# A decoder layer on one core: prompt scores in plain fp32, and four smaller edits on TensorE's way

## The chip, the cores and the metric

The kernel runs on one core of a Trainium2 chip. The metric is the device time of one execution in microseconds (us). A core has the engines TensorE (PE; its weight loads are listed as PEld), VectorE (DVE), ScalarE (ACT), GpSimd (POOL) and SyncE (SP); the last two here mostly issue DMAs. PSUM is the memory that PE writes to, SBUF the one that it reads from.

## What is computed

One layer of a hybrid decoder over 256 prompt rows and 8 x 8 sample rows (T = 320 rows in all), D = 2048, in fp32:

```python
xn = rms_norm(x, g_mix)
z = xn @ w_in                      # B, C, h, q, k, v, gate_conv, gate_attn
u = C * h;  y_A = (B * conv3(u)) @ w_conv_out
s = (q . k) * HEAD_DIM**-0.5 + rel_bias[t5_bucket(dist)]    # 16 heads, 4 key heads, window 128
p = softmax(s with a sink per head);  y_B = (p . v) @ w_attn_out
h = x + (sigmoid(gate_conv) * y_A + sigmoid(gate_attn) * y_B) @ w_o
h = h + (silu(hn @ w_gate) * (hn @ w_up)) @ w_down          # hn = rms_norm(h, g_ffn), D_FF = 5632
y = rms_norm(h, g_final)
```

It also returns the last keys and values and the state of the convolution.

## The kernel before, in words

Activations lie with features on the partitions and the 320 rows along the free axis. Each weight arrives by SP in blocks of 512 KB (`wraw`), ACT rounds it to fp32r (`whi`), and DVE takes the difference (`wlo`; `split_to`, L127 to L130). A product is then three fp32r matmuls: high by high, high by low, low by high (`product`, L176). The moving rows are read in a turned order, four at a time (`turns`, L101); the order in which the three kinds follow each other is set by `passes`.

Work beside the products comes from a generator, `side_work`, which takes one step after each weight block (`tick`), and from a list, `pending`, whose entries are put behind a block's split and matmuls.

The places that the change touches, in the order of the program:

- *The norms' sums.* `two_rows` splits a row of sums of squares into two fp32r parts and `over_partitions` (L197 to L199) adds them over the partitions with two matmuls, both with the weights `ones_r` and both in the turned order: into `prb` for the first norm, into `pss` for the second. A `nudge` (L193 to L195) is a matmul whose result nobody uses; it reads its rows in one piece. One follows the second norm's sum by way of `pending`, two stand in the sample attention, one in the first product.
- *Prompt scores.* `keys_twice` (L773) writes high and low parts of each key head to both halves of the partitions (`k2`), and `q_out` (L793) writes for each query chunk two tiles, with the high part on one half and the low part on the other (`q2`, in `at_t`). `prompt_scores` (L537) then makes, for a key head and two query heads (one of 8 `units`), six fp32r matmuls of 256 columns over all 128 partitions (L548 and L551) into `ps1` and `ps0`, and DVE adds the bias. `prompt_weights` (L627) runs the units two ticks apart.
- *First 128 rows of the output.* In the second half of the last product, `down` (L1023) makes three columns of 512 features: per weight set (two chunks of 128) eight matmuls of 512 columns `dn` with `whi`, two rows `dl` for the low part of the first 128 activations, and eight matmuls of 320 columns with `wlo`. Afterwards `rows_of` (L1120) turns the first 128 rows of a column by four PE transposes (`fa`, L1124), adds the low part `ylow`, sums squares and multiplies by `gfb`; `rest_of` takes the other 192 rows. Both are put in `pending` behind each column.
- *Last column.* Its weights are held. L1178 to L1200 make the products of the other rows, 384 columns with `whi` (L1191) and 320 with `wlo` (L1196), and every second set takes an entry of `pending`. DVE then adds the results (L1212, L1213, L1219, L1224) and sums squares into `yacc` (L1217, L1220). The first 128 rows are made with rows as weights, into `rowacc` (L1231); between them stand `pn` (L1235), which sums `yacc` over the partitions, and four transposes of `hT` (L1238). From `pn` ACT and DVE make the factor and seven products (L1248) for the output of the other rows, and from `rowacc` those of the first.

Of the kernel before, what the change touches and what calls it, by code (L numbers as in the profile page):

```python
# [21 lines left out]
WIN = 128  # L22
# [30 lines left out]
def hybrid_layer(ctx: ExitStack, tc: tile.TileContext, a: dict, o: list):  # L53
# [133 lines left out]
    def two_rows(src, hi, lo):  # L187

        nc.scalar.activation(hi, fives(src), AF.Copy)
        nc.vector.tensor_sub(lo, fives(src), hi.bitcast(F32))  # L190
        return hi, lo
# [240 lines left out]
    def first_norm():  # L432
# [5 lines left out]
        parts = two_rows(xacc, at_h(7), at_l(7))  # L438
# [37 lines left out]
    k2 = pr.tile([P, NKV, 2, TP], F32R, name="k2")  # L476
    k2h, k2l = k2[:, :, 0], k2[:, :, 1]

    def q2(ch, par):
        o = LEAD_A + ch * at_row + par * TP  # L480
        return at_t[:, o:o + TP]

# [54 lines left out]
    def prompt_scores(kv, gp, bias):  # L537

        j, par = kv // 2, kv % 2
# [15 lines left out]
        p0 = ps0.rearrange("p (g two k) -> p g two k", g=2, two=2)  # L558
        nc.vector.tensor_add(s[:, 0:2], p0[:, :, 0], flip(bias[:, :, 0:WIN]))
        nc.vector.tensor_add(s[:, 0:2], p0[:, :, 1], s[:, 0:2])  # L560
# [66 lines left out]
    def prompt_weights(scrs):  # L627
        bias, sc, sm = {}, {}, {}
        bias[0] = bias_load(*units[0])
        for i in range(len(units) + 1):  # L630
            if i < len(units):
                if i + 1 < len(units):
                    bias[i + 1] = bias_load(*units[i + 1])
                sc[i] = prompt_scores(*units[i], bias.pop(i))
                yield
                sm[i] = prompt_softmax(*units[i], sc[i])
# [136 lines left out]
    def keys_twice():  # L773
        for kv in range(NKV):
# [563 lines left out]
```

## Time and profile before

| | us |
|---|---|
| median of 3 runs | 1594.37 (1593.99 to 1594.84) |
| the profiled execution | 1594.48 |
| its span, first to last instruction | 1592.8 |
| PE busy | 1584.2 (99%), 11296 matmuls, granted clock 0.998 |
| DVE, ACT, POOL busy | 882.6 (55%), 650.2 (41%), 125.3 (8%) |
| DMA | 166 GB/s in the mean |

Busy time of PE is counted from modelled ends of pipelined matmuls, so that neighbours overlap; the time from one start to the next is the price of a matmul in a row. A plain fp32 matmul leaves two records in the trace, an fp32r one leaves one.

### The profile page before, as it was taken

The page shows a single profiled execution, that of the slowest core. Times are in us where ns is not written, and L with a number is a line of the kernel's source. Part 1 is how long each engine was busy: PE and PEld are TensorE (multiplying, and loading weights), DVE is VectorE, ACT ScalarE, POOL GpSimd, SP SyncE. Part 2 cuts the span into 40 slices and gives each one's busy share as a digit, 9 for nine tenths or more (in the row PEclk, how much of TensorE's full clock was granted, in tenths as well). Part 3 has the DMA queues.
Part 4 walks back from the last instruction along what each step waited for, and adds up shares of the span by engine and source line. Part 5 has one row for each costly group of instructions (what it writes and reads, how often), then busy time and mean ns, then how long its engine had stood idle before and what let it go on. Part 6 is the DMA issues. An engine that isn't in the chain of part 4 may idle for free.

```text
span 1592.8 us, 27120 instructions
## 1 busy us (share of the span) xinstructions
PE 1584.2 (99%) x11296; PEld 1569.0 (99%) x11296; DVE 882.6 (55%) x1258; ACT 650.2 (41%) x901; POOL 125.3 (8%) x214
## 2 busy tenths in 40 slices
PE   9999999999999999999999999999999999999998
PEld 9999999999999999999999999999999999999887
DVE  7889765455444455565555555553444455555556
ACT  7555344333333333444333333333333343344443
POOL 2223342000000003320000000000000000000000
PEclk9999999999999999999999999999999999999999
DMA  8666666444444444444444444455555544445652
GB/s 274 205 188 194 214 188 217 156 156 158 159 159 154 157 157 156 159 159 156 156 155 157 159 159 159 155 153 158 158 159 159 159 155 156 155 158 159 185 173 93
DMA packets 77090, 264.51 MB, mean 166 GB/s; under 512 B 9576, under 2 KB 13000, under 8 KB 76840
## 3 DMA queue, kind: packets, MB, share of 16 engines
q1 hardware_dynamic: 71880, 249.86, 49.3%
q0 software_dynamic: 4656, 12.25, 2.5%
q8 instruction: 88, 1.44, 0.4%
q10 hardware_dynamic: 432, 0.69, 0.1%
q14 instruction: 34, 0.28, 0.1%
HBM read 256.46 MB, written 8.26 MB: 166 GB/s over the span
## 4 chain that ended last, share of the span: by engine, by line
PE 99%; ACT 0%; DVE 0%; DVEq 0%; issue 0%
PE fu L176 19%; PE fg L176 19%; PE dn L1015 12%; PE wo L176 7%; PE ga L176 7%; PE gc L176 7%; PE q L176 3%; PE B L176 3%; PE H L176 3%; PE C L176 3%; PE ya L176 3%; PE yc L176 3%; PE dn L1040 3%; PE dn L1048 2%; PE kv L371 2%; PE dl L1044 1%
## 5 line engine op out<-in xcount | busy, mean ns | idle before, releaser
L130 DVE TENSOR_TENSOR wlo<-wraw,whi 128x1024 fp32r<-128x1024 f32 (+1 forms) x460 | 562.4, 1223 | 580.1 <-ACT whi L129 569.4
L129 ACT ACTIVATE whi<-wraw 128x1024 fp32r<-128x1024 f32 (+1 forms) x460 | 485.1, 1056 | 713.0 <-PE fu L176 131.9
L176 PE MATMUL fu<-hh_t,whi 128*128 128x320 f32 x704 | 205.1, 301 | 0.0
L176 PE MATMUL fu<-hl_t,whi 128*128 128x320 f32 x704 | 205.0, 301 | 0.0
L176 PE MATMUL fg<-hh_t,whi 128*128 128x320 f32 x704 | 205.0, 301 | 0.0
L176 PE MATMUL fg<-hl_t,whi 128*128 128x320 f32 x704 | 205.0, 301 | 0.0
L1015 PE MATMUL dn<-a_t,whi 128*128 128x320 f32 x896 | 162.6, 301 | 0.0
L176 PE MATMUL fu<-hh_t,wlo 128*128 128x320 f32 x704 | 158.8, 301 | 0.0
L176 PE MATMUL fg<-hh_t,wlo 128*128 128x320 f32 x704 | 158.8, 301 | 0.0
L1015 PEld LDWEIGHTS dn<-a_t,whi 128*128 128x128 f32 x896 | 137.5, 187 | 0.0
L176 PEld LDWEIGHTS fu<-hl_t,whi 128*128 128x128 f32 x704 | 131.7, 187 | 0.0
L176 PEld LDWEIGHTS fu<-hh_t,whi 128*128 128x128 f32 x704 | 131.6, 187 | 0.0
L176 PEld LDWEIGHTS fg<-hh_t,whi 128*128 128x128 f32 x704 | 131.6, 187 | 0.0
L176 PEld LDWEIGHTS fg<-hl_t,whi 128*128 128x128 f32 x704 | 131.6, 187 | 0.0
L176 PEld LDWEIGHTS fu<-hh_t,wlo 128*128 128x128 f32 x704 | 116.1, 187 | 0.0
L176 PEld LDWEIGHTS fg<-hh_t,wlo 128*128 128x128 f32 x704 | 116.1, 187 | 0.0
L1015 PE MATMUL dn<-a_t,wlo 128*128 128x320 f32 x448 | 103.9, 301 | 0.0
L1015 PEld LDWEIGHTS dn<-a_t,wlo 128*128 128x128 f32 x448 | 74.8, 187 | 0.0
L176 PE MATMUL gc<-xh_t,whi 128*128 128x320 f32 x256 | 74.5, 301 | 0.0
L176 PE MATMUL gc<-xl_t,whi 128*128 128x320 f32 x256 | 74.5, 301 | 0.0
L176 PE MATMUL ga<-xh_t,whi 128*128 128x320 f32 x256 | 74.5, 301 | 0.0
L176 PE MATMUL ga<-xl_t,whi 128*128 128x320 f32 x256 | 74.5, 301 | 0.0
(319 smaller groups left out, 2811.0 us busy)
## 6 DMA issues: line engine op xcount, KB each, us to landing
wraw<-in_w_in_dram SPq DMA_DIRECT2D x128, 512.0 KB, 3.7
wraw<-in_w_gate_dram SPq DMA_DIRECT2D x88, 512.0 KB, 3.6
wraw<-in_w_up_dram SPq DMA_DIRECT2D x88, 512.0 KB, 3.6
wraw<-in_w_down_dram SPq DMA_DIRECT2D x88, 512.0 KB, 3.6
wraw<-in_w_o_dram SPq DMA_DIRECT2D x32, 512.0 KB, 3.6
wraw<-in_w_conv_out_dram SPq DMA_DIRECT2D x16, 512.0 KB, 3.7
wraw<-in_w_attn_out_dram SPq DMA_DIRECT2D x16, 512.0 KB, 3.7
wraw<-in_w_kv_dram SPq DMA_DIRECT2D x6, 512.0 KB, 7.7
```

What stands on the lines that cost most here:

```text
L129: last["hi"] = nc.scalar.activation(hi, src, AF.Copy)
L130: last["lo"] = nc.vector.tensor_sub(lo, src, hi.bitcast(F32))
L176: last["mm"] = nc.tensor.matmul(turns(fives(ps[c][:, :T])), w[:, k, c * P:(c + 1) * P], turns(x(kc)), start=(kc == 0 and i == 0), stop=(kc ...
L371: last["mm"] = nc.tensor.matmul(turns(fives(ps[c][:, :T])), w[:, k, c * P:(c + 1) * P], turns(x(kc)), start=(kc == 0 and m == 0), stop=(kc ...
L1015: last["mm"] = nc.tensor.matmul(turns(fives(ps[c][:, :T])), parts[k][w][:, c * P:(c + 1) * P], turns(x(k)), start=k == 0 and m == 0, stop= ...
L1040: nc.tensor.matmul(turns(placed(ps[c])), parts[k][0][:, cs], turns(a_move(k)), start=k == 0, stop=False)
L1044: nc.tensor.matmul(low, a_low(k), parts[k][0], start=k == 0, stop=k == nf - 1)
L1048: last["mm"] = nc.tensor.matmul(turns(placed(ps[c])[:, :, 0:JT]), parts[k][1][:, cs], turns(a_move(k)[:, :, 0:JT]), start=False, stop=k == ...
```

## The change

- `over_partitions` reads the low part in one piece, from a plain stretch of 320 columns that is lent by `at_t` or `a_t` (`a_fives` returns it as a third value). The `nudge` behind the second norm goes.
- The prompt scores become plain fp32. `q_out` writes the scaled query once (`qf`), `keys_twice` goes (four empty steps keep the others in place), and `prompt_scores` makes two key heads at once: the heads lie on partitions 0 to 63 and 64 to 127 of `kT` and `qf`, their matmuls alternate and go to separate PSUM tiles. Four groups of eight matmuls take the place of eight groups of six. `prompt_biased` adds the bias, and a `nudge` follows the last group one tick later.
- `rows_turn` turns the first 128 rows of a column on DVE in blocks of 32 and takes them through DRAM by five POOL DMAs (four writes of 64 KB, one read of 256 KB) straight to `y0`; `rows_of` only adds `ylow`. The columns of `ylow`, `g_final` and the output are permuted to match, the last two on the host. `pending` gets three entries a column, and the last column takes one at every even set.
- In the last column all sets but the final one run all matmuls with `whi` first and then those with `wlo`.

```diff
     def two_rows(src, hi, lo):
...
-        nc.vector.tensor_sub(lo, fives(src), hi.bitcast(F32))
+        nc.vector.tensor_sub(fives(lo), fives(src), hi.bitcast(F32))
...
     def over_partitions(out, parts):
-        for i, x in enumerate(parts):
-            nc.tensor.matmul(turns(fives(out)), ones_r, turns(x), start=i == 0, stop=i == 1)
+        hi, lo = parts
+        nc.tensor.matmul(turns(fives(out)), ones_r, turns(hi), start=True, stop=False)
+        nc.tensor.matmul(out, ones_r, lo, start=False, stop=True)
...
-        parts = two_rows(xacc, at_h(7), at_l(7))
+        parts = two_rows(xacc, at_h(7), at_t[:, LEAD_A + 6 * at_row:LEAD_A + 6 * at_row + T])
...
-    def prompt_scores(kv, gp, bias):
...
-        ps1, ps0 = ps_aux(u("ps1")), ps_aux(u("ps0"))
-        for gi in range(2):
-            q = q2(j * 4 + gp * 2 + gi, par)
-            for i in range(2):
-                nc.tensor.matmul(
-                    ps1[:, gi * 256:(gi + 1) * 256], q[:, WIN:2 * WIN], k2[:, kv, i], start=i == 0, stop=i == 1
-                )
-            nc.tensor.matmul(
-                ps0[:, gi * 256:(gi + 1) * 256].rearrange("p (two k) -> p two k", two=2), q[:, 0:WIN],
-                k2[:, kv, :, 0:WIN], start=True, stop=True,
-            )
+    def prompt_scores(j, gp):
+
+        both = [(ps_aux(u("ps1")), ps_aux(u("ps0"))) for _ in range(2)]
+        for gi in range(2):
+            q = qf[:, j * 4 + gp * 2 + gi]
+            for b, n in ((0, WIN), (1, 2 * WIN)):
+                for par, (ps1, ps0) in enumerate(both):
+                    rows = slice(par * 64, par * 64 + 64)
+                    nc.tensor.matmul(
+                        (ps1 if b else ps0)[:, gi * n:(gi + 1) * n], q[rows, b * WIN:(b + 1) * WIN],
+                        kT[rows, j, 0:n], start=True, stop=True,
+                    )
+        return both
...
         for i in range(len(units) + 1):
             if i < len(units):
...
+                if i % 2 == 0:
+                    both[i], both[i + 1] = prompt_scores(units[i][0] // 2, units[i][1])
+                sc[i] = prompt_biased(*both.pop(i), bias.pop(i))
+                if i + 2 < len(units):
+                    bias[i + 2] = bias_load(*units[i + 2])
                 yield
+                if i == len(units) - 2:
+                    nudge(xh, xl, T)
                 sm[i] = prompt_softmax(*units[i], sc[i])
...
-        yield from keys_twice()
+        for _ in range(4):
+            yield
...
-            t = tmp("ta", "qt")[:, :TP]
-            nc.vector.tensor_mul(t, ps[c][:, :TP], rbq[:, :TP])
-            for par in range(2):
-                r0, o0 = par * 64, 64 - par * 64
-                q = q2(j * 4 + g, par)
-                nc.scalar.activation(q[r0:r0 + 64], t[r0:r0 + 64], AF.Copy)
-                nc.vector.tensor_sub(q[o0:o0 + 64], t[r0:r0 + 64], q[r0:r0 + 64].bitcast(F32))
+            nc.vector.tensor_mul(qf[:, j * 4 + g], ps[c][:, :TP], rbq[:, :TP])
...
-        nc.scalar.activation(ylow[:, c0:c0 + 512], low, AF.Copy)
+        nc.scalar.activation(
+            ylow[:, c0:c0 + 512].rearrange("p (a k j) -> p k a j", a=4, k=4),
+            low.rearrange("p (k a j) -> p k a j", k=4, a=4), AF.Copy,
+        )
...
-                over_partitions(pss[:, :T], two_rows(hacc, a_hi(FH[0] - 1), a_lo(FH[0] - 1)))
+                over_partitions(pss[:, :T], two_rows(hacc, a_hi(FH[0] - 1), a_spare))
                 rstd_of(pss[:, :T], [P, T], "r2", hp, out=rb2)
-                pending.append(lambda: nudge(hh, hl, P))
...
+            def rows_turn(c0):
+
+                flipped = op.tile([P, 512], F32, tag="jk", name=u("yT")).rearrange("p (b k j) -> p b k j", b=4, k=4)
+                nc.vector.transpose(
+                    flipped.rearrange("p b k j -> p k b j"),
+                    hT[:, c0 // P:c0 // P + 4, 0:P].rearrange("p k (b i) -> p k b i", i=B),
+                )
+                rows = turned_rows(f"y_scr{c0}", flipped.rearrange("p b k j -> p (b k j)"), 4, 4 * B)
+                nc.gpsimd.dma_start(y0[:, c0:c0 + 512], rows)
+
             def rows_of(c0):
 
-                pt = ps_aux(u("fa"))
-                for c in range(4):
-                    nc.tensor.transpose(pt[:, c * P:(c + 1) * P], hT[:, c0 // P + c, 0:P], ident)
                 y = y0[:, c0:c0 + 512]
-                nc.vector.tensor_add(y, pt, ylow[:, c0:c0 + 512])
+                nc.vector.tensor_add(y, y, ylow[:, c0:c0 + 512])
...
                 down(c0)
+                pending.append(lambda c0=c0: rows_turn(c0))
+                pending.append(lambda c0=c0: rest_of(range(c0 // P, c0 // P + 4)))
                 pending.append(lambda c0=c0: rows_of(c0))
-                pending.append(lambda c0=c0: rest_of(range(c0 // P, c0 // P + 4)))
...
-        for k, c, m in passes(order, end):
+        for k, c, m in passes(order, end) if end else [(k, c, m) for m in (0, 2) for k, c in order]:
...
-        if pending and i % 2 == 1:
+        if pending and i % 2 == 0:
```

The change also moves rows. On PE, at the first scores, in the product `C` (`ps` are the PSUM tiles of the scores, `k` is `k2`), there stood before

```order
L176 MATMUL C_1138<-xh_t,wlo_1142 128x16x5x4
L548 MATMUL ps_134_1188<-k_496,at_t 128x256 x2
L551 MATMUL ps_135_1189<-k_496,at_t 128x256
L548 MATMUL ps_134_1188<-k_496,at_t 128x256 x2
L551 MATMUL ps_135_1189<-k_496,at_t 128x256
L176 MATMUL C_1137<-xh_t,whi_1203 128x16x5x4
```

and now

```order
L176 MATMUL C_1092<-xh_t,wlo_1096 128x16x5x4
L540 MATMUL ps_126_1132<-kT,qf 128x128
L540 MATMUL ps_128_1134<-kT,qf 128x128
L540 MATMUL ps_125_1131<-kT,qf 128x256
L540 MATMUL ps_127_1133<-kT,qf 128x256
L540 MATMUL ps_126_1132<-kT,qf 128x128
L540 MATMUL ps_128_1134<-kT,qf 128x128
L540 MATMUL ps_125_1131<-kT,qf 128x256
L540 MATMUL ps_127_1133<-kT,qf 128x256
L176 MATMUL C_1091<-xh_t,whi_1152 128x16x5x4
```

so that a group holds two heads, and the place of every second group is empty.

On DVE, behind the last weight splits (`xv` holds `hT`, `ya` is `y0`, `dn` are the last column's results), there stood before

```order
L130 TENSOR_TENSOR wlo_15883<-wraw_15880,whi_15882 128x1024
L1126 TENSOR_TENSOR ya<-fa_15922,ylow 128x512
L1144 TENSOR_TENSOR yacc<-yacc,sq_15963 128x192
L1144 TENSOR_TENSOR yacc<-yacc,sq_15967 128x192
L1128 TENSOR_TENSOR ya<-ya 128x512
L1144 TENSOR_TENSOR yacc<-yacc,sq_15971 128x192
L1204 TENSOR_REDUCE s_16043<-ssf 128x1
L1144 TENSOR_TENSOR yacc<-yacc,sq_15975 128x192
L1205 TENSOR_SCALAR s_16043<-s_16043 128x1
L1206 TENSOR_SCALAR h_16044<-s_16043 128x1
L1212 TENSOR_TENSOR xv<-xv,dn_15886 128x192
L1213 TENSOR_TENSOR xv<-xv,dn_15886 128x192
```

and now

```order
L130 TENSOR_TENSOR wlo_15809<-wraw_15806,whi_15808 128x1024
L1109 STREAM_TRANSPOSE yT_15832<-xv 128x4x4x32
L1137 TENSOR_TENSOR yacc<-yacc,sq_15872 128x192
L1137 TENSOR_TENSOR yacc<-yacc,sq_15876 128x192
L1137 TENSOR_TENSOR yacc<-yacc,sq_15880 128x192
L1137 TENSOR_TENSOR yacc<-yacc,sq_15884 128x192
L1206 TENSOR_TENSOR xv<-xv,dn_15812 128x192
L1119 TENSOR_TENSOR ya<-ya,ylow 128x512
L1207 TENSOR_TENSOR xv<-xv,dn_15812 128x192
L1213 TENSOR_TENSOR xv<-xv,dn_15812 128x128
L1206 TENSOR_TENSOR xv<-xv,dn_15813 128x192
L1121 TENSOR_TENSOR ya<-ya 128x512
```

so that the sum with `ylow` and the product with `gfb` (and three small rows behind them) have moved in between the adds of the last column, and the sum stands behind a read from DRAM.

On PE, behind the last column's products, there stood before

```order
L1231 MATMUL rowacc<-a_t_13016 128x512 x8
L1235 MATMUL pn<-yacc,ones_r 128x192
L1238 MATMUL rowacc<-ident,xv 128x128 x4
L1231 MATMUL rowacc<-a_t_13016 128x512 x4
L1231 MATMUL rowacc<-more,a_t_13016 128x512 x8
```

and now

```order
L1225 MATMUL rowacc<-a_t_12936 128x512 x8
L1232 MATMUL rowacc<-ident,xv 128x128 x4
L1225 MATMUL rowacc<-a_t_12936 128x512
L1229 MATMUL pn<-yacc,ones_r 128x192
L1225 MATMUL rowacc<-a_t_12936 128x512 x3
L1225 MATMUL rowacc<-more,a_t_12936 128x512 x8
```

so that the four transposes and one row product come ahead of `pn`.

## Rows read from the trace of the kernel before

**Rows 1.** The page's part 4: the chain that ended last, by engine

```profile
PE 99%; ACT 0%; DVE 0%; DVEq 0%; issue 0%
```

**Rows 2.** PE by stretch: from:to, length, busy (instructions), granted clock, DMA share, GB/s

```profile
39.39:90.59 51.20, 51.20 (x362) 1.00 0.61 194
90.59:91.29 0.70, 0.70 (x8) 1.00 0.69 217
218.55:221.68 3.13, 3.13 (x24) 1.00 0.57 178
708.28:711.69 3.41, 3.41 (x26) 1.00 0.45 154
712.00:912.00 200.00, 200.00 (x1430) 1.00 0.49 157
```

**Rows 3.** PE in order of time, prompt values: start us, us, engine, line, what

```profile
197.66 0.60 PE L612 MATMUL po<-side,vn 128*64 128x256 f32 x4
198.09 1.03 PE L612 MATMUL po<-pT,vn 128*64 128x256 f32 x8
```

**Rows 4.** PE in order of time, at the sample scores

```profile
215.66 0.58 PE L176 MATMUL B<-xh_t,wlo 128*128 128x320 f32 x3
216.17 2.06 PE L684 MATMUL pss<-kf,qs 64*32 64x136 f32 x64
...
218.55 0.30 PE L176 MATMUL B<-xh_t,whi 128*128 128x320 f32 x1
```

**Rows 5.** PE in order of time, at the nudge behind the second norm

```profile
711.70 0.22 PE L195 MATMUL nudge<-hh_t,hl_t 128*128 128x128 f32 x1
...
711.95 0.30 PE L176 MATMUL fu<-hl_t,whi 128*128 128x320 f32 x1
```

**Rows 6.** The chain that ended last, from the last column on: start us, us, what

```profile
1556.53 0.67 PE dn L1191 x4
...
1561.54 0.44 PE fa L1124 x4
...
1572.08 0.68 PE dn L1191 x4
...
1577.04 1.85 PE rowacc L1231 x8
```

**Rows 7.** DVE in order of time, behind the last split: [idle before <- releaser]

```profile
1565.52 0.68 DVE L1126 TENSOR_TENSOR ya<-fa,ylow 128x512 f32<-128x512 f32 x1
1566.12 0.74 DVE L1144 TENSOR_TENSOR yacc<-yacc,sq 128x192 f32<-128x192 f32 x2
...
1568.34 0.15 DVE L1205 TENSOR_SCALAR s<-s 128x1 f32<-128x1 f32 x1
...
1573.36 0.35 DVE L1212 TENSOR_TENSOR xv<-xv,dn 128x192 f32<-128x192 f32 x1 [4.69 <-PE dn L1196]
...
1574.60 0.36 DVE L1212 TENSOR_TENSOR xv<-xv,dn 128x192 f32<-128x192 f32 x1 [0.30 <-PE dn L1196]
...
1578.25 0.36 DVE L1220 TENSOR_TENSOR yacc<-yacc,sq 128x192 f32<-128x192 f32 x1
...
1582.39 3.77 DVE L1248 TENSOR_TENSOR wraw<-xv,rnr 128x576 f32<-128x576 f32 x7
```

**Rows 8.** Tile `T`, prompt weights turned and written: ns min/median/max; landing of the writes

```profile
L265 POOL DMA_DIRECT2D p_scr<-T x32: 552/552/596, 105.0 to 155.2; - x32
L590 DVE STREAM_TRANSPOSE T<-s x8: 695/709/714, 104.0 to 152.6; 128x512 f32<-128x512 f32 x8
...
DMA to landing us min/median/max: 1.9/3.9/5.5
```

**Rows 9.** Tile `pT`, the same weights read back from DRAM: landing

```profile
DMA to landing us min/median/max: 3.2/4.7/5.4
```

**Rows 10.** All engines in one stretch of the last column; DMA share and GB/s stand last

```profile
1568.00:1572.00 4.00, 4.00 (x28) 4.00 (x27) 0.60 (x4) 0.16 (x1) 0.00 (x0) 1.00 0.00 0
```

**Rows 11.** Tile `dl`: ns min/median/max, first and last start us

```profile
L1044 PE MATMUL dl<-whi,a_t x48: 388/391/396, 1474.8 to 1551.2; 128*128 128x512 f32 x48
```

More of the change, by code (lines that the diff above doesn't have):

```diff
@@ L472, in hybrid_layer @@
     pr = pr_p.enter_context(tc.tile_pool(name="pr", bufs=1, side="right"))
[L476 to L481, printed above, removed]
+    qf = pr.tile([P, 8, TP], F32, name="qf")
     def kv_turn(t):
@@ L557, in prompt_scores @@
         nc.vector.tensor_max(s[:, 2:4], w[:, :, 0:WIN], w[:, :, WIN:2 * WIN])
-        p0 = ps0.rearrange("p (g two k) -> p g two k", g=2, two=2)
-        nc.vector.tensor_add(s[:, 0:2], p0[:, :, 0], flip(bias[:, :, 0:WIN]))
-        nc.vector.tensor_add(s[:, 0:2], p0[:, :, 1], s[:, 0:2])
+        nc.vector.tensor_add(
+            s[:, 0:2], ps0[:, 0:2 * WIN].rearrange("p (g k) -> p g k", g=2), flip(bias[:, :, 0:WIN])
+        )
         return s
@@ L627, in prompt_weights @@
     def prompt_weights(scrs):
-        bias, sc, sm = {}, {}, {}
-        bias[0] = bias_load(*units[0])
+        bias, both, sc, sm = {}, {}, {}, {}
+        for i in range(2):
+            bias[i] = bias_load(*units[i])
         for i in range(len(units) + 1):
             if i < len(units):
-                if i + 1 < len(units):
-                    bias[i + 1] = bias_load(*units[i + 1])
-                sc[i] = prompt_scores(*units[i], bias.pop(i))
+                if i % 2 == 0:
[3 more added lines that the diff above has]
+                    bias[i + 2] = bias_load(*units[i + 2])
                 yield
+                if i == len(units) - 2:
+                    nudge(xh, xl, T)
                 sm[i] = prompt_softmax(*units[i], sc[i])
@@ L771, in sample_attention @@
             yield
-    def keys_twice():
-        for kv in range(NKV):
-            j, r0 = kv // 2, kv % 2 * 64
-            src = kT[r0:r0 + 64, j, 0:TP]
-            for o0 in (r0, 64 - r0):
-                nc.scalar.activation(k2h[o0:o0 + 64, kv, :], src, AF.Copy)
-            for o0 in (r0, 64 - r0):
-                nc.vector.tensor_sub(k2l[o0:o0 + 64, kv, :], src, k2h[r0:r0 + 64, kv, :].bitcast(F32))
-            yield
     def kv_work():
@@ L976, in a_fives @@
         groups = [rows_in(flat, LEAD_C + g * group, step, lambda k: k % per * JS) for g in range(4)]
-        return [lambda k, i=i: groups[2 * i + k // per](k) for i in range(2)]
+        spare = flat[:, LEAD_C + 2 * group:LEAD_C + 2 * group + T]
+        return *(lambda k, i=i: groups[2 * i + k // per](k) for i in range(2)), spare
     def parts_of(row):
@@ L1068, in hybrid_layer @@
         if half == 0:
-            a_hi, a_lo = a_fives()
+            a_hi, a_lo, a_spare = a_fives()
         else:
@@ L1301 @@
     vec = _np.concatenate([_np.asarray(inputs[n]).reshape(-1, P) for n in ("g_mix", "g_ffn", "w_conv", "g_final")])
+    g_last = _np.asarray(inputs["g_final"]).reshape(-1)
+    inputs["g_final"] = _np.concatenate([g_last[:E0].reshape(-1, 4, 4, B).swapaxes(1, 2).reshape(-1), g_last[E0:]])
     inputs["x_v"] = _np.concatenate([vec.T[:, :16], by_feature(x).reshape(P, -1), vec.T[:, 16:]], axis=1)
@@ L1334 @@
     rest = _np.asarray(res[1]).transpose(2, 1, 0).reshape(T - P, D)
+    rows = _np.asarray(res[0])
+    res[0] = _np.concatenate([rows[:, :E0].reshape(P, -1, 4, 4, B).swapaxes(2, 3).reshape(P, E0), rows[:, E0:]], axis=1)
     res[:2] = _np.concatenate([res[0], rest[:TP - P]])[None], rest[TP - P:].reshape(NB, TS, D)
```

3 lines of the change are left out of this document (2 added, 1 removed).

## The prediction

> **What bounds the kernel now.** I read the page first, then the step of TensorE from one matmul to the next, then each place that the diff touches. In the page's chain that ended last, TensorE (PE) holds 99% and everything else rounds to nothing [rows 1]. So an edit that only lightens VectorE (DVE), ScalarE (ACT) or a queue is worth nothing before the last microseconds; what counts is the number of matmuls, the price of each, and what is read after the last of them.
>
> The price is not one number. In the view of all PE instructions by stretch [rows 2], divide each length by the count less two (two were still running at the stretch's front edge): 200/1428 = 140.1 ns from matmul to matmul in the long stretch, but 51.2/360 = 142.2 ns between the first norm's matmuls (39.4 us) and the first scores (90.6 us), 3.13/22 = 142.3 ns after the sample scores and 3.41/24 = 142.1 ns after the second norm's matmuls. The granted clock is 1.00 (2.4 GHz) in each, so it is not the clock. I call these the quick and the slow gait; the slow one costs 2.2 ns a matmul. Two of the three stretches begin at `over_partitions`, whose matmuls read their rows in the turned order; each ends at matmuls that read fp32r rows in one piece: the scores at 90.59, a `nudge` at 221.68 and one at 711.70 [rows 5].
>
> **The sum, part by part** (positive is slower).
>
> *Scores.* Before, a unit is six fp32r matmuls in 0.70 us (six by the same count) [rows 2]; eight units, 5.60 us. After, four groups of eight plain fp32 matmuls. A plain fp32 matmul has two records in the trace. The nearest priced row is the product with the values, 256 wide, two side by side: from 197.66 to 198.09 four records, two matmuls, in 0.43 us [rows 3]; 128 wide would be half. If two key heads on different halves of the partitions go side by side in the same way, a group is 2 x (0.43 + 0.215) = 1.30 us. Going in and out of such a burst has a price: the sample scores, which also use 64 rows, take from 215.66 to 218.55 together with five ordinary matmuls (three before, two after, 0.70 us) [rows 4]; eight rounds of 136 columns at 0.43 x 136/256 = 0.23 us are 1.83 us, which leaves 0.36. So 4 x 1.66 = 6.64 us against 5.60: **+1.04**. Bounds: nothing for going in and out, -0.4; not side by side, a rival below.
>
> *Gait after the scores.* After the sample scores (64 rows, read in one piece) the gait is slow [rows 2]. I take the same for the new bursts, from the first to the new nudge: 13 side turns of 24 matmuls, 312 x 2.2 ns = +0.69, and the nudge itself: one of 128 columns takes 0.25 - 0.14 = 0.11 from 711.70 to 711.95, where it stands with one matmul [rows 5]; 192 columns more are 0.08 at 2.4 a ns. **+0.88**; the lower bound is +0.19, if the gait stays quick.
>
> *First norm.* The second matmul of `prb` now reads one piece, as all that ended a slow gait did: 360 x 2.2 ns = **-0.79**.
>
> *Second norm.* The same for 24 matmuls, -0.05, and its nudge goes, 0.11. **-0.16**.
>
> *Turning the first rows.* Three groups of four transposes leave PE, 0.44 us each on the chain [rows 6]: **-1.32**. The DVE transposes that replace them (0.71 us for this size [rows 8]) and the sums stand between weight splits. In the second and third columns of `down` I cost them at nothing: four splits lie between a transpose and the sum that needs its rows, and a split follows PE at one set, about 3.4 us (eight products at 0.23, eight at 0.14, two low rows at 0.23), so 13.5 us, while the trip through DRAM takes 0.71, three further issues at 0.55, 3.9 and 4.7 at the medians, 11 us [rows 8, 9]. If that cover went, the three weight buffers would still hold two sets.
>
> *Last products by width.* The first 96 of the last column take 1572.08 - 1556.53 - 0.44 = 15.11 us, 157.4 ns each, with widths mixed; the last 32, in blocks of four, 4.96 us, 155.0 ns [rows 6]. In blocks of eight I take 155: 96 x 2.4 ns = **-0.23**. The waits of this stretch are on data long there; nothing new stands behind them.
>
> *The end.* Here a DVE row costs time. Before, from the first add of the last column (1573.36) to `yacc` (1578.61) DVE works without a gap but for 0.3 us [rows 7], and PE's `pn` stands behind eight row products that take 1.85 from 1577.04 [rows 6], 0.3 after that row's end. In the changed order five rows move between: the sum with `ylow` and the product with `gfb` (0.6 us from start to start; the sum stood at 1565.52), and three small ones of `s3`, 0.2 each by the 0.15 of one [rows 7]: 1.8 us, less the 0.3. Moving the four transposes and a row product ahead of `pn` gives PE something to do meanwhile, but the way to the end leads from `pn` through ACT and seven DVE products (to 1586.2 [rows 7]), so I count nothing back. **+1.5**.
>
> The sum with `ylow` also waits for the last rows from DRAM. The transpose takes the place of the row at 1565.52 [rows 7], to 1566.23; its writes follow; the fourth write is issued at 1568.0; the DMA engines are idle then [rows 10], so I take the fastest landings, 1.9 for a write and 3.2 for a read [rows 8, 9]: 1573.1, and 0.1 for two handovers. It is wanted at 1573.0 (0.67 sooner than before, the transposes' 0.44 and the 0.23 above). **+0.2**; by the medians +3.6, by the slowest 5.5 and 5.4 +5.9, below nothing.
>
> A rule bears on that wait. The Trainium skill, "DMA: Bandwidth & Descriptors", section "Anatomy of one DMA — SWDGE (gpsimd) path", prices such a transfer at 2.0 us plus its bytes at 436 KB per us; as an estimate 2.15 for a write of 64 KB and 2.6 for the read of 256 KB. By it the rows are there at 1572.8 and the 0.2 goes. The loaded medians, 3.9 and 4.7, differ from it; no row of before shows this path with idle engines.
>
> Sum: 1.04 + 0.88 - 0.79 - 0.16 - 1.32 - 0.23 + 1.5 + 0.2 = +1.12 us. The profiled execution took 1594.48 (span 1592.8 and 1.7 around it), 0.1 above the median of 1594.37. Forecast: 1594.4 + 1.1 = **1595.5 us**.
>
> **Rivals.**
> 1. *The slow gait is not ended by `over_partitions`.* What turned the gait may be the weights `ones_r`, which stay, not the turned rows. Then nothing clears it after the second norm, since the nudge is gone, until the first one-piece matmul of `down` at 1474.8 [rows 11]: 766 us / 0.140 = 5470 matmuls x 2.2 ns = +12.0, and the first norm's 0.79 isn't won: 1608.3, slower. It decides as soon as a flat read with those weights leaves the gait slow. Against it: after the nudge at 711.70 the gait is quick [rows 2], as the fall of 2 ns a matmul shows.
> 2. *The two heads don't go side by side.* They use different rows but all columns of the array; the rows of before show sharing only where columns differ too. In full that is 4 x 1.30 = +5.2: 1600.7. The Trainium skill, "TensorE: Matmul & The Clock Gate", section "Measured speedup vs the span model", has four row tiles at 3.07 times one, 77% of full sharing; by that, an estimate, the bursts would be 1.69 us and the sum 1.6 higher. No run here shows it yet.
> 3. *The last rows come late*, at loaded prices: +3.4 on the forecast, 1598.9.
> 4. *The end is free and the gait quick after the scores*: DVE's rows overlap better than I add them, -1.7, and -0.69: 1593.1.
> 5. *Faster by more than I can sum*: all gains with scores and end at their lower bounds give 1594.4 - 0.4 + 0.19 - 0.79 - 0.16 - 1.32 - 0.23, 1591.6; more would need a stall that PE doesn't have.
>
> **How the numbers follow.** A measurement of this kernel can tell about 0.2% from no change, 3.2 us: below 1591.2 is faster, above 1597.6 slower. Chances: the forecast with its smaller bounds 0.58, rival 4 0.14, rival 3 0.11 (half of it above 1597.6), rival 2 0.07 (two thirds of it above), rival 1 0.08, rival 5 0.02. Same: 0.58 + 0.14 + 0.05 + 0.02 = 0.79 less 0.02 for what I didn't see = 0.77. Slower 0.19, faster 0.04. The range leaves out rival 1, the full price of rival 2 and the worst of rival 3: 1592.2 to 1599.0.
>
> **What would show it.** A score group of 1.3 us from its first to its last start and about 0.35 more around it; 140 ns from 39.4 to 90.6 and after 708; no `fa` rows; `pn` idle for about a microsecond before it, and DVE's sum with `ylow` within half a microsecond of its turn. 142 ns in the long stretch would prove rival 1; 2.6 us a group, rival 2; DVE waiting several microseconds for the rows near 1571, rival 3. A gap of PE inside `down` would contradict the cover that I claimed there.

## The result: 0.13% slower, no change by the bound of the prediction

| | before | after |
|---|---|---|
| median of 21 runs | 1594.37 (1593.61 to 1594.94 without one run) | 1596.49 (1594.97 to 1597.52) |
| ratio, 95% interval | | 1.0013 (1.0007 to 1.0019) |
| span of the profiled execution | 1592.8 | 1594.3 |

One run of the kernel before took 4207 us; it hardly moves the median, and nothing here shows what it was. The change costs 2.1 us by the medians and 1.5 by the profiles. The forecast was 1595.5 with "same" as the likeliest; its sum of +1.1 is 1.0 short, and one of its terms was wrong in kind. On the page TensorE still holds the chain that ended last, though less of it than in [rows 1]; DVE and DMA have come in:

```profile
PE 98%; DVE 1%; DMA 1%; issue 0%; ACT 0%; POOL 0%; DVEq 0%; POOLq 0%; ACTq 0%
```

Between landmarks that both kernels have on PE (each length is the difference of two start times), in us:

| from, to | before | after | difference | forecast |
|---|---|---|---|---|
| start, first norm's sum | 39.11 | 39.07 | -0.04 | 0 |
| first norm's sum, first scores | 51.48 | 50.78 | -0.70 | -0.79 |
| first scores, product with the values | 106.59 | 109.22 | +2.63 | +1.92 |
| product with the values, first `dl` | 1277.58 | 1277.42 | -0.16 | -0.16 |
| first `dl`, last column | 81.61 | 80.74 | -0.87 | -0.88 |
| last column, its last product | 20.37 | 19.77 | -0.60 | -0.67 |
| last product, `pn` | 1.99 | 3.26 | +1.27 | +1.7 |
| `pn`, end | 14.04 | 13.98 | -0.06 | 0 |

Two places decide, the scores and the end. First PE by stretch in the changed kernel (from:to, length, busy and count, granted clock, DMA share, GB/s), beside [rows 2]:

```profile
39.40:89.62 50.22, 50.22 (x360) 1.00 0.63 197
92.06:104.79 12.73, 12.73 (x93) 1.00 0.50 148
141.00:147.31 6.31, 6.31 (x47) 1.00 0.38 114
149.07:198.84 49.77, 49.77 (x351) 1.00 0.69 224
...
712.00:912.00 200.00, 200.00 (x1431) 1.00 0.49 157
```

Lengths go by the count less one or two, as many as were still running at the front edge; step by step the trace has 140 or 142 ns in the same stretches. Behind the first norm the gait is now quick (50.22/359 = 139.9 ns), and so it is behind the bursts of scores (12.73/91 = 139.9), against the forecast. But from 149 to 199 us the gait is slow: 49.77/350 = 142.2 ns at a granted clock of 1.00.

A burst, in order of time on PE, beside [rows 3, 4]; a plain fp32 matmul leaves two records:

```profile
89.34 0.58 PE L176 MATMUL C<-xh_t,wlo 128*128 128x320 f32 x3
89.86 1.58 PE L540 MATMUL ps<-kT,qf 64*128 64x128 f32 x16
91.37 0.41 PE L176 MATMUL C<-xh_t,whi 128*128 128x320 f32 x1
```

From the first score to the next product are 1.51 us. Going in costs 0.09 (the step into the burst is 0.23 instead of 0.14), going out 0.13 (the next four steps are 0.248, 0.147, 0.147 and 0.149): 1.73 a group.

Then what starts the slow stretch: the view of waits from 138 to 150 us (who, for whom: us, times, longest), and ACT and PE in order of time there.

```profile
ACT s L569 <- DVE mx L562: 6.6, 1, 6.6
...
DVE wlo L130 <- ACT whi L129: 3.0, 1, 3.0
PEld H L176 <- ACT whi L129: 0.2, 1, 0.2
PEld nudge L195 <- DVE s L551: 0.2, 1, 0.2
```

```profile
135.50 1.04 ACT L129 ACTIVATE whi<-wraw 128x1024 fp32r<-128x1024 f32 x1
143.16 0.40 ACT L569 ACTIVATE s<-s,mx 128x128 f32<-128x128 f32 x1 [6.62 <-DVE mx L562]
...
146.46 2.94 ACT L129 ACTIVATE whi<-wraw 128x1024 fp32r<-128x1024 f32 x3
```

```profile
146.89 0.72 PE L176 MATMUL C<-xh_t,wlo 128*128 128x320 f32 x4
147.56 0.42 PE L176 MATMUL H<-xh_t,whi 128*128 128x320 f32 x1
...
148.82 0.42 PE L176 MATMUL H<-xh_t,wlo 128*128 128x320 f32 x1
149.07 0.30 PE L176 MATMUL H<-xh_t,whi 128*128 128x320 f32 x1
```

ACT stands 6.6 us before the softmax of the last two units, whose exponentials follow each other without a split between them; the three splits due meanwhile come in a row from 146.46. PE's weight load waits for the first, and its steps around 147.3 and 148.8 are 0.245, 0.252, 0.157 and 0.252 instead of 0.14: 0.35 us lost, and behind it the slow gait, 356 x 2.2 ns = 0.78. The `nudge` at 140.47 waits too, for DVE to free its PSUM tile: with its neighbours it costs 0.35. What is left of the +2.63, 1.15, is the bursts (four at 1.73, less the entry into the first, less eight units of before at 0.71).

At the end, DVE in order of time, beside [rows 7]:

```profile
1566.65 0.70 DVE L1109 STREAM_TRANSPOSE yT<-xv 128x512 f32<-128x512 f32 x1
...
1573.63 0.35 DVE L1206 TENSOR_TENSOR xv<-xv,dn 128x192 f32<-128x192 f32 x1 [4.27 <-PE dn L1190]
1574.62 0.69 DVE L1119 TENSOR_TENSOR ya<-ya,ylow 128x512 f32<-128x512 f32 x1 [0.63 <-DMA ya<-y_scr]
...
1576.10 0.69 DVE L1121 TENSOR_TENSOR ya<-ya 128x512 f32<-128x512 f32 x1
...
1579.78 0.36 DVE L1214 TENSOR_TENSOR yacc<-yacc,sq 128x192 f32<-128x192 f32 x1
```

The sum with `ylow` waits 0.63 us for the rows from DRAM; it, the product by `gfb` and the small rows stand between the adds. Ten of the profiles have this end as changed, and in each the length from the last product to `pn` less this wait is 2.63 to 2.65 us: so the rows cost 0.64 against the 1.99 of before, and the wait is paid in full. The chain shows the trip (start us, us, what):

```profile
1567.64 1.62 POOL y_scr L266 x3
1569.27 1.98 DMA y_scr<-yT
1571.32 0.49 issue
1571.83 2.77 DMA ya<-y_scr
```

The last write took 1.98 us and the read 2.77, behind the last weight load. The Trainium skill, "DMA: Bandwidth & Descriptors", section "Anatomy of one DMA — SWDGE (gpsimd) path", gives 2.15 and 2.6 by its formula, as an estimate. This trace agrees to 0.2 us, and so do the reads of the ten profiles to 0.4 (2.75 to 3.00); of their last writes nine took 1.96 to 1.99 and one 2.76. The trips of the two columns before, beside weight loads, took 3.6 to 5.2 for a write and 3.3 to 5.5 for a read.

### The profile page after: what moved, and what is told of

It reads as the page before. It is cut to its first block, busy times and chain, and to the rows that moved or that the text cites. A ratio compares the mean times of both kernels' runs of the same rounds, so it can differ in the third digit from the quotient of the medians.

```text
span 1594.3 us, 27113 instructions
## 1 busy us (share of the span) xinstructions
PE 1584.8 (99%) x11300; PEld 1567.3 (98%) x11300; DVE 871.9 (55%) x1229; ACT 639.2 (40%) x877; POOL 132.6 (8%) x229
## 4 chain that ended last, share of the span: by engine, by line
PE 98%; DVE 1%; DMA 1%; issue 0%; ACT 0%; POOL 0%; DVEq 0%; POOLq 0%; ACTq 0%
PE fu L176 19%; PE fg L176 19%; PE dn L999 12%; PE wo L176 7%; PE ga L176 7%; PE gc L176 7%; PE H L176 3%; PE B L176 3%; PE C L176 3%; PE q L176 3%; PE ya L176 3%; PE yc L176 3%; PE dn L1024 3%; PE kv L372 2%; PE dn L1032 2%; PE dl L1028 1%
## 5 line engine op out<-in xcount | busy, mean ns | idle before, releaser
L176 PE MATMUL wo<-m_l,whi 128*128 128x320 f32 x256 | 74.5, 301 | 0.0
L176 PE MATMUL wo<-m_h,whi 128*128 128x320 f32 x256 | 74.5, 301 | 0.0
```

The lines of the kernel that those rows point to most:

```text
L176: last["mm"] = nc.tensor.matmul(turns(fives(ps[c][:, :T])), w[:, k, c * P:(c + 1) * P], turns(x(kc)), start=(kc == 0 and i == 0), stop=(kc ...
```

## The experiments

Each starts from the changed kernel. The kernel before, run on the same chips, had medians of 1594.48 (first four), 1594.43 (next four) and 1594.10 (last four). In the tables "scores" is the length from the first scores to the product with the values (before 106.59, changed 109.22), "tail" that from the last product to `pn` (1.99 and 3.26).

### Where the time is: scores, last column

The scores of before in the changed kernel (`prompt_scores`, `prompt_weights`, `q_out`, `keys_twice`, `k2` and `q2` as in the diff's minus lines):

> The changed kernel with the fp32r scores of before (k2, q2, two heads after each other, no nudge behind them); everything else as changed. The trace of the changed kernel loses 2.63 us between the first scores and the product with the values. Theory A, all of it comes with the scores (four bursts +1.04, a nudge of 0.35, two stalls of PE near 147 and 149 us, and 142 ns instead of 140 from there to 199 us): 2.6 us below the changed kernel, about 1593.9, gait 140 ns from 39 to 215 us, no stall at 147. The forecast's terms (+1.04 and +0.88): 1.9 below. Rival, the loss sits in the end of the kernel and the scores are even: no difference, 1596.5.

The third column turned by PE again:

```diff
             def rows_of(c0):
+                if c0 == E0 - 512:
...
+                    for c in range(4):
+                        nc.tensor.transpose(pt[:, c * P:(c + 1) * P], hT[:, c0 // P + c, 0:P], ident)
...
-                pending.append(lambda c0=c0: rows_turn(c0))
+                if c0 < E0 - 512:
+                    pending.append(lambda c0=c0: rows_turn(c0))
```

> The changed kernel, but the first 128 rows of the third column (the last that is turned) go through four PE transposes as before; the first two columns stay with DVE and DRAM. Theory, the forecast's: in the end DVE's moved rows and the wait for the last rows from DRAM cost (traced: 1.27 us between the last product of the last column and pn); with this edit PE pays 0.44 for the transposes, and pn starts 1.2 sooner after the last product: 0.8 us below the changed kernel, 1595.7, and the sum with ylow waits for nothing. Rival: the end is bound by something else (sums of squares, the products by the factor), and only the 0.44 is left: 1596.9. The spread of the changed kernel's single runs (1595.0 to 1597.5, before 1593.6 to 1594.9) would shrink to before's if the trip through DRAM makes it.

| | median, us | scores | tail |
|---|---|---|---|
| scores as before | 1594.12 (1593.31 to 1595.26) | 106.60 | 4.03 |
| last column by PE | 1594.89 (1594.05 to 1596.02) | 108.52 | 1.99 |

With the old scores the 2.6 us are gone (2.4 by the medians), so they do come with the scores. The tail of that execution is longer still: the last of its four writes took 2.76 us instead of 1.98, and the sum with `ylow` waited 1.39 instead of 0.63. So the wait differs from one execution to the next: 0.45 to 0.77 in nine of the ten profiles, 1.39 in this one.

With PE on the last column the tail is that of before to 0.01 us, and PE pays the transposes: 20.20 us from the start of the last column to its last product against 19.77, 0.43 more. The order of the last products alone is then 20.20 - 20.37 = -0.17. The profile's gain at the end is the 0.84 expected (1.27 - 0.43). The median gained 1.6, and not all of it is accounted for: this profile also had the quick gait from 150 to 199 us, 0.70 less at the scores, and 0.43 more ahead of the first norm's sum, so that the two profiled executions differ by 1.1; the other 0.5 lies between the changed kernel's median and its profiled execution. The single runs still spread over 2.0 us, so the trip alone does not make the spread. The chain of this kernel, to be held against [rows 6]:

```profile
1576.87 0.56 PE dn L1201 x4
1577.43 1.85 PE rowacc L1236 x8
1579.28 0.37 PE pn L1240 x2
```

### What starts the slow gait: the nudge and the stall

```diff
-                if i == len(units) - 2:
-                    nudge(xh, xl, T)
```

> The changed kernel without the nudge behind the fourth group of scores. Theory 1 (an interruption of PE starts the slow gait, the score bursts do not): 140 ns from the last burst to the stall at 147 us, 142 from there to 199 as in the changed kernel, and the nudge's 0.35 us saved: 1596.1. The forecast's theory 2 (the bursts leave the slow gait, the nudge ends it): 142 ns from the last burst at 139 us on, 60 matmuls by 2.2 ns more, 0.13, less 0.35: 1596.3. The times lie too near; the gait between 139 and 147 us decides.

The next kernel makes the same nudge at `i == len(units)`, behind the second `yield`:

> The changed kernel with that nudge moved some four ticks later, behind the two stalls of PE at 147.3 and 148.8 us. Theory 1 (the stalls start the slow gait, a read in one piece ends it): 142 ns only from 147.5 to the nudge near 154, 140 from there to 199, 316 matmuls by 2.2 ns or 0.70 us less, and the nudge no longer waits for its PSUM tile, 0.11 to 0.19 instead of 0.35: 1595.6. Rival (the slow gait there has another cause, such as the product H or the work beside it): 142 ns goes on behind the nudge, 1596.3 to 1596.5.

| | median, us | scores | gait 150 to 199 us |
|---|---|---|---|
| no nudge | 1596.20 (1594.92 to 1597.39) | 108.50 | quick |
| nudge later | 1595.81 (1595.32 to 1596.43) | 108.73 | slow to 155.1, then quick |

PE by stretch without the nudge, then with the later one:

```profile
137.80:147.12 9.32, 9.32 (x68) 1.00 0.42 135
149.60:198.20 48.60, 48.60 (x349) 1.00 0.70 229
```

```profile
149.51:154.90 5.39, 5.39 (x39) 1.00 0.65 207
155.20:198.70 43.50, 43.50 (x313) 1.00 0.70 229
```

Behind the bursts the gait is quick (in the first of these stretches each step in the trace is 140 ns): the forecast's theory 2 falls. Theory 1 falls in half: there was a stall without the nudge too, and this time the gait behind it was quick. In nine of the profiles PE stalls near 148 us; five then go on slow (142.2 ns) and four quick (140.0); in the five without a stall there the gait is quick. The later nudge ends a slow gait (43.50/311 = 139.9). Its eleven runs lie within 1.1 us where the changed kernel's 21 spread over 2.6, which fits a chance taken out but does not show it: the kernel with the scores of before has no such stall, and its eleven spread over 2.0.

Without the nudge's wait ahead of it the stall grew: one step of 0.65 instead of 0.25. The weights of `H` are rounded 57.7 us after the first scores in all three kernels. The nudge's wait only hid a part of ACT's lateness.

### ACT's order

```diff
-                sm[i] = prompt_softmax(*units[i], sc[i])
+                if i % 2 == 0:
+                    sm[i] = prompt_softmax(*units[i], sc[i])
             yield
+            if i < len(units) and i % 2:
+                sm[i] = prompt_softmax(*units[i], sc[i])
```

> The changed kernel with the softmax of every second unit issued one tick later, so that on ACT two weight splits stand between the exponentials of the two heads, where the changed kernel has all eight exponentials and then the splits. Theory (the two softmaxes in a row hold up the next whi, PE stalls for it near 147 and 149 us, and that throws the gait): no stall there, 140 ns from the nudge to the product with the values, 0.35 us of stalls and in about half of the executions 0.78 of slow gait less: about 1595.7, with runs closer together. Rival (the stall has its cause in the weights' arrival or in DVE): stall and lottery remain, 1596.5.

1596.39 us (1596.04 to 1597.97), scores 109.53: not the 1595.7 expected, and no gain. The waits from 136 to 150 us in this kernel, and ACT in order of time:

```profile
ACT s L569 <- DVE mx L562: 7.4, 2, 6.2
...
PE nudge L195 <- DVE s L551: 1.4, 1, 1.4
```

```profile
144.34 0.40 ACT L569 ACTIVATE s<-s,mx 128x128 f32<-128x128 f32 x1 [6.24 <-DVE mx L562]
...
146.00 2.00 ACT L129 ACTIVATE whi<-wraw 128x1024 fp32r<-128x1024 f32 x2
```

The stalls at 147 and 149 are gone and the steps from 142 to 199 us are 140 ns. That does not show ACT's order to be their whole cause. DVE now reaches the bias adds of the last group (L551) at 141.24 instead of 140.00, and the nudge, which needs a PSUM tile that these adds free, holds PE for 1.5 us; so PE comes to `H` 59.0 us after the first scores instead of 57.7. The split that it needs there ends at 57.4, only 0.3 sooner than before, since ACT still stands 6.2 us waiting for DVE. Without the hold, an estimate from these times, PE would have come to `H` at 57.25 and waited about 0.2 us, where the kernel without the nudge waited 0.5. One wait went and another took its place; the version without this nudge was not run, and how much of the stall is ACT's order and how much DVE's stays open.

### The two heads

```diff
-        for gi in range(2):
...
-                for par, (ps1, ps0) in enumerate(both):
+        for par, (ps1, ps0) in enumerate(both):
...
+            for gi in range(2):
```

> The changed kernel with the eight matmuls of a score group in another order: the four of one key head, then the four of the other, so that neighbours use the same rows of the array. Theory (in the changed kernel the two heads share the time in full): a group takes twice its 1.27 us, 2.5, and the four groups together cost 5.1 us more: 1601 to 1602. Rival (the pairs of records 5 to 7 ns apart are only how the trace writes them, and the heads gain nothing from the alternation): 1.27 us a group as before, 1596.5.

1597.82 us in one timed execution. PE at the first group:

```profile
90.03 2.34 PE L540 MATMUL ps<-kT,qf 64*128 64x128 f32 x16
92.30 0.41 PE L176 MATMUL C<-xh_t,whi 128*128 128x320 f32 x1
```

A group takes 2.27 us instead of 1.51, four groups 3.0 more, not the 5.1 expected. The alternation does make the heads share the time: by a factor of 1.50 where 2 is full. The Trainium skill, "TensorE: Matmul & The Clock Gate", section "Measured speedup vs the span model", has 3.07 of 4 for four row tiles of 32 rows, 77%. These two tiles of 64 rows reach 75%, near it. (The single run is only 1.3 over the changed kernel since it met neither the stalls nor the slow gait: scores 110.89, which is 1.67 over 109.22; 3.0 less 0.78, 0.35 and 0.2 of the nudge's wait.)

### Which reads bring the slow gait: the second norm

Both of its matmuls turned, no nudge:

```diff
+    def both_turned(out, parts):
+        for i, x in enumerate(parts):
+            nc.tensor.matmul(turns(fives(out)), ones_r, turns(x), start=i == 0, stop=i == 1)
...
-                over_partitions(pss[:, :T], two_rows(hacc, a_hi(FH[0] - 1), a_spare))
...
+                both_turned(pss[:, :T], (a_hi(FH[0] - 1), lo))
```

> The changed kernel with both matmuls of the second norm's sum turned, as before, and without the nudge that stood behind them before. Theory 1 (a wait of PE on its operands throws the gait anew, quick or slow, and a read in one piece that does not itself wait brings the quick one): nothing clears the gait from 710 us to the first rows dl at 1476, so where it is thrown slow 5470 matmuls pay 2.2 ns, 12.0 us, 1608.5; in other executions it may fall quick, 1596.5. Theory 2 of the forecast (the turned reads themselves start the slow gait): 142 ns in that stretch in every execution, 1608.5. Rival (the nudge and the flat read of the second norm do nothing; the weights ones_r or the change of products sets the gait): 140 ns throughout, 1596.5.

And the first read in one piece, the second turned:

```diff
+        nc.tensor.matmul(out, ones_r, hi, start=True, stop=False)
+        nc.tensor.matmul(turns(fives(out)), ones_r, turns(lo), start=False, stop=True)
```

> The changed kernel with the second norm's two matmuls in the other order of reading: the first, which waits for ACT, reads one piece, the second turned rows. Theory 1 (only a flat read that does not wait ends a slow gait): as with both turned, 1608.5 where the gait is thrown slow, 1596.5 where quick. Theory 2 (the form of the last read decides): slow in every execution, 1608.5. Rival (any read in one piece will do): 140 ns, 1596.5 in every execution.

| | median, us | 710 us to the first `dl` |
|---|---|---|
| both turned | 1608.81 (1608.32 to 1609.07, 4 runs) | 142.2 ns |
| one piece first | 1595.95 (1595.05 to 1596.86) | 140.0 ns |

```profile
711.10:1489.00 777.90, 777.90 (x5471) 1.00 0.49 155
```

```profile
710.20:1475.00 764.80, 764.80 (x5465) 1.00 0.50 157
```

777.90/5470 = 142.2 and 764.80/5464 = 140.0 ns, both at a granted clock of 1.00. Two turned reads with `ones_r` brought the slow gait in every execution, though PE waited for nothing there (the steps are 140, 143, 143 ns); it then stayed for 778 us and cost 12.3 us over the changed kernel. One read in one piece is enough for a quick gait behind the norm, and it may be the first of the two. Theory 1 loses the first kernel (no wait, yet slow), theory 2 the second. In both the gait was quick ahead of the norm (140 ns), and so it was ahead of both norms in the kernel before: what these kernels show is that two turned reads start the slow gait, not yet that a one-piece read of a norm ends one.

### Stalls on purpose

```diff
+        for _ in range(copies):
+            nc.scalar.activation(hi[:, :n, :], raw[:, :n, :], AF.Copy)
...
+        late = half == 0 and k0 == 8 and fpair in (2, 5, 8, 11)
+        return load_cols(w_g, k0, n, c0, copies=8 * late)
```

> The changed kernel with four weight blocks of the gate product made late on purpose (pairs 2, 5, 8 and 11, near 765, 845, 925 and 1005 us): ACT writes the rounded block eight times over before the real one, so that PE waits some 3 us for its weights at each. Theory 1b, as the runs so far leave it (a wait of PE for weights throws the gait, quick or slow by chance; the two turned reads of a norm always give the slow one): behind each stall 142 or 140 ns, changing from stall to stall and from run to run; a slow stretch costs 1.3 us between two stalls and 7.4 from the last to 1476, so single runs spread over several us above 1596.5 plus four stalls. Theory 2 (turned reads of over_partitions and bursts alone change the gait): 140 ns behind every stall, and a spread of some 2 us as in the changed kernel.

The second kernel adds a nudge behind each late block:

```diff
+        if late:
+            pending.append(lambda: nudge(hh, hl, P))
```

> The same four late blocks, each followed by a nudge of 128 columns read in one piece behind the block's matmuls. Theory 1b: at most the 48 matmuls of that block are slow, behind each nudge 140 ns; single runs lie within some 2 us of each other, and lie at the lower end of the runs with stalls alone, plus 4 x 0.11 us. Theory 2: no difference to the stalls alone but those 0.44 us.

1620.28 us (1619.38 to 1622.54) and 1621.84 (1617.80 to 1624.71). PE by stretch at the second stall of the first kernel:

```profile
841.90:846.70 4.80, 1.76 (x11) 0.94 0.00 0
846.70:852.90 6.20, 6.17 (x23) 0.50 0.59 177
853.00:930.00 77.00, 77.00 (x543) 1.00 0.47 150
```

and between the nudges of the second kernel:

```profile
767.40:843.00 75.60, 75.60 (x542) 1.00 0.47 152
851.90:929.00 77.10, 77.10 (x543) 1.00 0.48 158
939.00:1016.00 77.00, 77.00 (x543) 1.00 0.47 153
1024.70:1476.00 451.30, 451.30 (x3175) 1.00 0.51 157
```

Without nudges the gait behind the four stalls was quick, slow (77.00/541 = 142.3), quick, quick: not the same behind each, as theory 1b expected. With nudges the opposite of what was expected: quick after the first, slow after the other three. Step by step, the gait was quick ahead of those three nudges, and slow some four steps behind them. A nudge of 128 columns does not bring the quick gait; it changed it, in the kernel before from slow to quick [rows 5], here from quick to slow. The 320-column nudges are another matter: 44 of them, in all the profiles, that did not wait themselves had the quick gait behind them, 21 of them with a slow one ahead. So had 24 of 25 norms with a one-piece read, but in 21 of the 25 the gait was quick ahead of the norm too; out of a slow gait three of four came out quick, and in one profile (below) the slow gait stayed. Of eight nudges that waited, all with a quick gait ahead, seven had a quick one behind them and one a slow one.

### The last rows earlier, and all of it together

```diff
-                pending.append(lambda c0=c0: rows_turn(c0))
+                if c0 < E0 - 512:
+                    pending.append(lambda c0=c0: rows_turn(c0))
...
+        if j == 5:
+            with after(last["lo"]):
+                rows_turn(E0 - 512)
```

> The changed kernel, but DVE turns the rows of the third column between the splits of the last weights, some 4 us sooner, instead of behind the last split; the trip through DRAM, the sum with ylow and the product by the factor then lie ahead of the last column's adds. Theory (the end's loss is the moved DVE rows and the wait for the trip, which lasts a different time in each execution): pn starts 2.0 us after the last product as before instead of 3.3, PE pays no transposes: 1.3 to 1.6 below the changed kernel, 1594.9 to 1595.2, and its runs lie closer together. Rival (the rows cost DVE the same wherever they stand, and delay the last splits and so PE): pn 2.0 behind, but PE stalls in the last column by about 0.7, 1595.9.

> The fp32r scores of before and the early turning of the last rows together, with the rest of the change (both norms' flat reads, no fa transposes, last products by width). If the parts add up: against the kernel before -0.78 (first norm) -0.16 (second norm) -1.30 (three groups of transposes) -0.17 (width) and nothing at the end, 2.4 less: 1592.0. If the end costs as in the changed kernel (1.3): 1593.3.

| | median, us | scores | tail |
|---|---|---|---|
| last rows early | 1595.07 (1593.84 to 1595.98) | 109.21 | 2.00 |
| the same, scores of before | 1592.65 (1592.30 to 1593.31) | 106.60 | 2.23 |

Turned between the splits, at 1563.3 instead of 1566.7, the rows are back before the last column's adds begin, and the tail is that of before without transposes on PE. The median gains 1.4, as expected; its runs spread over 2.1 us, so that they lie closer together is not shown. Its profile happens to be one with the slow gait behind the first norm, which the one-piece read did not end, and again from 150 us on:

```profile
39.80:90.70 50.90, 50.90 (x360) 1.00 0.62 192
```

With the scores of before the kernel beats both: ratio 0.9989 to the kernel before, interval 0.9980 to 0.9998, 0.1% and inside the bound that the prediction calls the same. The chain of its end runs through a read from DRAM of 4.62 us, where the changed kernel's took 2.77, to `pn`:

```profile
1559.70 0.72 DVE yT L1127
...
1564.88 4.62 DMA ya<-y_scr
1569.53 0.70 DVE ya L1137
...
1571.02 0.69 DVE ya L1139
...
1572.15 0.27 DVE xv L1228
...
1576.33 0.37 DVE yacc L1236
...
1576.74 0.59 PE pn L1251 x2
```

The sum with `ylow` (L1137) and the product by `gfb` (L1139) stand ahead of the adds on DVE, so that the late rows push the adds (L1228), and `pn` starts 0.24 later than in the kernel before: even started early, the trip is not free when its read is that long. By the profile it gains 1.9 (span 1590.8), by the medians 1.8; the 2.4 expected lost 0.24 at the tail and 0.2 before the first norm, in the stretch whose length differs between executions anyway (38.9 to 39.7 us to the first norm's sum).

## Why the prediction was right, and where not

**Right for its number, by terms that partly made up for each other.** The time lies in the range, 1.0 above the forecast, and the verdict is the likeliest one. In the profile the scores came out 0.7 above their forecast and the end 0.4 below it; that the sum is so near is in part luck. 0.5 of the 1.0 is between the changed kernel's median and its profiled execution (1594.3 and 1.7 around it). What makes this 0.5 is open: the trip is hardly it, since the profile's wait of 0.63 us lies in the middle of the ten; the stretch ahead of the first norm's sum, 39.07 us in this profile and 39.29 in the median of the others, gives 0.2. (By their own terms rival 3 adds 3.5 and rival 5 gives 1591.7; nothing rests on these tenths.)

*Confirmed to 0.1 us:* first norm (-0.70 for -0.79; the gait ahead of it was quick, so its sum no longer starts the slow gait, rather than ending one), second norm (-0.16), three groups of transposes (-1.30 for -1.32), last products by width (-0.17 for -0.23, shown by the kernel with PE on the last column). The cover claimed for the transposes inside `down` held: `dl` to last column lost the 0.87 and nothing came back.

*Scores.* The burst is 1.73 us for the 1.66 worked out from the rows of the values and the sample scores; going in and out is 0.22 for 0.36, the matmuls 1.51 for 1.30, and the two errors cancel in part. The heads do go side by side, but share 1.50 of 2 and not all, as in rival 2's milder form; in full that rival falls, and its price was too high: heads apart take 2.27 a group and not 2.60, 3.0 more and not 5.2.

*Gait after the scores: the step that failed.* "After the sample scores the gait is slow. I take the same for the new bursts." It is quick behind all four (139.9 ns); the sample scores, 64 by 32 of the array, say nothing of bursts of 64 by 128. The 0.78 of slow gait that stands in its place in the profile, from 149 to 199 us, is near the 0.69 by luck. It has another cause, which was not seen at all: the change has DVE and ACT treat two heads at a time, ACT stands 6.6 us for DVE and then has eight exponentials ahead of its next weight split, PE stalls 0.35, and behind this stall five of nine profiles go on slow. With the scores of before the stall and the slow gait are gone; how the stall is shared between DVE and ACT stays open. The nudge was priced from one that does not wait (0.19); it stands where DVE still holds its PSUM tile and cost 0.35. The prediction asked of the moved waits what is queued behind them on DVE at the end, and did not ask it of ACT here.

*The end.* +1.27 for +1.7, and the mechanism is shown: take the last column's trip away or start it earlier, and the tail is 1.99 and 2.00. The wait for the rows was 0.63 for 0.2, mainly because the transpose began at 1566.65 and not at 1565.5 (the split ahead of it waited for its weights); DVE's rows cost 0.64 for the 1.5 counted. In the ten profiles with this end as changed, the tail is 3.1 to 4.0, the longest with a wait of 1.39; rival 3, 3.4 more, did not come.

*Rival 1* fell for this kernel, and the kernel with both reads turned shows its price, 12.3 for 12.0. But the rule behind the forecast, that every one-piece read ends the slow gait, is too wide: three of four reads of 128 columns behind the late blocks started it, and one of the four norm reads that met it did not end it. *Rival 4's* quick gait came, its free end not.

## What to carry to other kernels

Read the step from one matmul to the next by stretch, even where the clock stands at full rate: 1.6% over half a kernel was decided by how one matmul reads its rows, and the gait can change at a place where PE waits for weights. Put a one-piece read as wide as the products behind such a place, where it need not wait itself, and look at the gait on both sides of it. When an edit pairs work that was spread, look at what the in-order engines then do in a row: the late one shows as somebody else's stall, and taking one wait away only lengthens the next as long as the pace is set elsewhere. A trip through DRAM at the end is free only if it is started early enough for its longest time, and if what waits for it does not stand ahead of other work on its engine.

## What the hardware showed that was not expected

- At a granted clock of 1.00 a 320-column fp32r matmul steps at 140.0 or at 142.2 ns, and keeps to it for hundreds of us (778 us and 5470 matmuls in one stretch). Two turned reads with the same weights, sample scores and stalls can start the slow one. What comes out can depend on what came in: the sample scores made a quick gait slow in 13 profiles, and in the one where it was slow ahead of them (the kernel with both reads turned, 142.3 ns) it was quick behind (140.1). What state this is stays open: the runs tell what changes it, not why a stall ends quick or slow.
- After two interruptions of PE, one step of 1.53 to 1.65 us and one of 2.0, with eight matmuls between, the records show steps of 267 ns and a granted clock of 0.50 (1.2 of 2.4 GHz) for 3 to 6 us, in five of the eight stalls made on purpose; in the other three the clock stayed at 1.00. So the times of those two kernels hold more than the gait, and only their traces, not their medians, speak for it.
- Two plain fp32 matmuls on different 64-row halves of the array share 1.50 of 2 in time.
